# First input transfers of one and three tiles, the third column's products in spare PSUM banks, and the gate's scaling by VectorE instead of GpSimd

## The chip, the cores and the metric

The kernel runs on one core of a Trainium2 chip. The metric is device time in microseconds (us), the median of several executions. One further execution is profiled, and all rows below are from it. Engines: PE is TensorE (matmul), PEld its weight load, DVE is VectorE, ACT is ScalarE, POOL is GpSimd, SP is SyncE, which here only issues DMAs. ACTq and SPq in a row are the sequencers that issue DMAs.

## What is computed

One layer of a streaming encoder, on 256 prompt tokens and 128 sample tokens, with a model width of 2048 and a feed-forward width of 5504 (43 columns of 128):

```python
def _swiglu(x, w_gate, w_up, w_down):
    return (jax.nn.silu(x @ w_gate) * (x @ w_up)) @ w_down
...
    x = x + 0.5 * _swiglu(_rmsnorm(x, p['norm_ffn1']), p['w_ffn1_gate'], p['w_ffn1_up'], p['w_ffn1_down'])
    m, ... = _mixer(_rmsnorm(x, p['norm_mix']), conv_buf, h_ssd, h5_re, h5_im, p)
    x = x + m
    x = x + 0.5 * _swiglu(_rmsnorm(x, p['norm_ffn2']), p['w_ffn2_gate'], p['w_ffn2_up'], p['w_ffn2_down'])
```

The mixer holds a state-space group (SSD) and an S5 group, whose small matrices are worked out from its parameters alone.

## The kernel before

All 384 tokens lie in the free dimension; a tile is 128 rows (of the width or of the weights) by 384 tokens, and the width of 2048 is 16 such tiles. To keep float32 precision each product is made of three: both operands are split into a high part (n_h, wh) and a low remainder (n_l, wl), and PE adds wh·n_h, wh·n_l and wl·n_h in one PSUM bank.

`split_unit` (L47) brings up to eight weight tiles: SP issues the transfer into `raw` (four buffers), ACT casts it to `wh` (L55), DVE subtracts to `wl` (L56), three buffers each. `linear` (L74) makes one output column of 128 rows from two such units, with the matmuls at L86 to L88, in a bank of the pool `psm` (four banks, "mm"). A second pool `psa` (four banks, "aux") serves sums of squares and the mixer.

`ffn` (L191) runs over the 43 columns in chunks of 11, 11, 11 and 10 (second feed-forward block: 15, 14, 14). For each column it makes the gate pg and the up product pu, then g = pg·r by DVE (L213), Silu by ACT (L214), g = g·r by POOL (L215), h = pu·g by DVE (L218), and the split of h into hh by ACT (L221) and hl by DVE (L222). After a chunk's columns the 16 down products pd follow. The scale r of the norm is not applied to x but here, since it is known only after all of x has been squared and summed; it comes from `rms` (L124), which the code calls behind column 0.

Column 0 of the first block is made by `first_pair` (L94), gate and up together, while x arrives: in pieces of 1, 1, 2, 4, 4, 4 of the 16 tiles it issues both weights' transfers on SP, then the transfer of as many x tiles by `feed1` (L1007; the first four tiles on ACT's queue, later ones on SP's), has ACT and DVE split x (L164, L165) and the weights (L108, L109), and issues six matmuls for each tile (L113, L115, L117).

With the second chunk the code interleaves side work, which the scheduler begins in the first chunk already: `s5_prepare` (L268): many small DVE operations (L243 to L265, L368 to L373, L420 to L428) and POOL operations that work out the S5 matrices and the table `ph`. It may start behind `late`, which is column 1's multiply on POOL; it begins with a transfer of the parameters `lam`.

The order on each engine is not that of the code: a scheduler sets it at build time from its own estimate of a timeline, and each engine then runs its list in that order.

Of the kernel before, what the change touches and what calls it, by code (L numbers as in the profile page):

```python
# [9 lines left out]
F32 = mybir.dt.float32  # L10
# [4 lines left out]
P = 128  # L15
D = 2048
T = 384
KT = D // P
# [28 lines left out]
def split_unit(c, wsrc, m, k0, nk):  # L47

    nc = c.nc
    raw = c.wst.tile([P, 8, P], F32, tag="raw", name=f"raw_{c.uid}", bufs=4)  # L50
    wh = c.wst.tile([P, 8, P], F32R, tag="wh", name=f"wh_{c.uid}", bufs=3)
    wl = c.wst.tile([P, 8, P], F32R, tag="wl", name=f"wl_{c.uid}", bufs=3)
    c.uid += 1
    nc.sync.dma_start(raw[:, :nk, :], wsrc[m, :, k0 : k0 + nk, :])
    nc.scalar.copy(wh[:, :nk, :], raw[:, :nk, :])  # L55
    nc.vector.tensor_sub(wl[:, :nk, :], raw[:, :nk, :], wh[:, :nk, :].bitcast(F32))  # L56
    return wh, wl


def turned(ap):  # L60

    return ap.rearrange("p (a b) -> p b a", a=2)


def halves(ap):
    return ap.rearrange("p (a b) -> p a b", a=2)


def straight(ps):

    return ps.rearrange("p (b a) -> p a b", a=2)


def linear(c, wsrc, m, k0, nk, xs, name):  # L74

    nc = c.nc
    ps = c.psm.tile([P, 512], F32, tag="mm", name=name)[:, :T]
    done = 0
    nu = -(-nk // 8)
    sizes = [nk // nu + (1 if i < nk % nu else 0) for i in range(nu)]  # L80
    for n in sizes:
        wh, wl = split_unit(c, wsrc, m, k0 + done, n)
        for i in range(n):
            xh, xl = (turned(z) for z in xs[done + i])
            first, last = done + i == 0, done + i == nk - 1
            nc.tensor.matmul(ps, wh[:, i, :], xh, start=first, stop=False)  # L86
            nc.tensor.matmul(ps, wh[:, i, :], xl, start=False, stop=False)  # L87
            nc.tensor.matmul(ps, wl[:, i, :], xh, start=False, stop=last)  # L88
        done += n
        c.tick()  # L90
    return ps


def first_pair(c, wa, wb, m, xs, names, feed):  # L94


    nc = c.nc
    pa, pb = (c.psm.tile([P, 512], F32, tag="mm", name=n)[:, :T] for n in names)
    k0 = 0
    for nk in (1, 1, 2, 4, 4, 4):  # L100
        raw = c.wst.tile([P, 2, 4, P], F32, tag="raw", name=f"raw_{c.uid}", bufs=4)
        wh = c.wst.tile([P, 2, 4, P], F32R, tag="wh", name=f"wh_{c.uid}", bufs=3)
        wl = c.wst.tile([P, 2, 4, P], F32R, tag="wl", name=f"wl_{c.uid}", bufs=3)
        c.uid += 1
        for i, w in enumerate((wa, wb)):
            nc.sync.dma_start(raw[:, i, :nk], w[m, :, k0 : k0 + nk, :])
        feed(k0, k0 + nk)
        last = nc.scalar.copy(wh[:, :, :nk], raw[:, :, :nk])  # L108
        nc.vector.tensor_sub(wl[:, :, :nk], raw[:, :, :nk], wh[:, :, :nk].bitcast(F32))  # L109
        for i in range(nk):  # L110
            xh, xl = (turned(z) for z in xs[k0 + i])
            for j, ps in enumerate((pa, pb)):
                nc.tensor.matmul(ps, wh[:, j, i, :], xh, start=k0 + i == 0, stop=False)  # L113
            for j, ps in enumerate((pa, pb)):
                nc.tensor.matmul(ps, wh[:, j, i, :], xl, start=False, stop=False)  # L115
            for j, ps in enumerate((pa, pb)):
                nc.tensor.matmul(ps, wl[:, j, i, :], xh, start=False, stop=k0 + i == KT - 1)  # L117
        k0 += nk
    for _ in range(4):
        c.tick()  # L120
    return pa, pb, last
# [69 lines left out]
def ffn(c, x, inp, wg, wu, wd, chunks, name, after, beside=None, before=None, feed=None):  # L191
    nc = c.nc
    r = late = None
    with c.tc.tile_pool(name=f"{name}_pool", bufs=1) as pool:
        f0 = 0
        for ci, nf in enumerate(chunks):
            if ci == 1 and beside:
                c.side.append(beside(late))
            hs = []
            for f in range(f0, f0 + nf):  # L200
                if f == 0 and feed:
                    pg, pu, last = first_pair(
                        c, wg, wu, f, inp.parts, (f"{name}_pg{f}", f"{name}_pu{f}"), feed
                    )
                    before(last)
                else:
                    pg = linear(c, wg, f, 0, KT, inp.parts, f"{name}_pg{f}")
                    pu = linear(c, wu, f, 0, KT, inp.parts, f"{name}_pu{f}")
                if r is None:
                    r = inp.scale(D)  # L210
                g = pool.tile([P, T], F32, tag="g", name=f"{name}_g{f}", bufs=2)
                h = pool.tile([P, T], F32, tag="h", name=f"{name}_h{f}", bufs=2)
                nc.vector.tensor_mul(halves(g), straight(pg), halves(r))  # L213
                nc.scalar.activation(g, g, AF.Silu)  # L214
                on_pool = nc.gpsimd.tensor_mul(g, g, r)  # L215
                if f == 1:
                    late = on_pool
                nc.vector.tensor_mul(halves(h), straight(pu), halves(g))  # L218
                hh = pool.tile([P, T], F32R, tag="hh", name=f"{name}_hh{f}", bufs=max(chunks) + 2)
                hl = pool.tile([P, T], F32R, tag="hl", name=f"{name}_hl{f}", bufs=max(chunks) + 2)  # L220
                nc.scalar.copy(hh, h)  # L221
                nc.vector.tensor_sub(hl, h, hh.bitcast(F32))  # L222
                hs.append((hh, hl))
            for m in range(KT):
                pd = linear(c, wd, m, f0, nf, hs, f"{name}_pd{ci}_{m}")
                xm = halves(x(m))
                nc.vector.scalar_tensor_tensor(xm, straight(pd), 0.5, xm, op0=ALU.mult, op1=ALU.add)
                if ci == len(chunks) - 1:
                    after(m)
            f0 += nf  # L230
        c.finish_side()
# [734 lines left out]
def trunk(ctx: ExitStack, tc: tile.TileContext, a, o):  # L966
    nc = tc.nc
    c = Ctx()
# [6 lines left out]
    c.psm = ctx.enter_context(tc.tile_pool(name="psm", bufs=4, space=bass.MemoryType.PSUM))  # L975
    c.psa = ctx.enter_context(tc.tile_pool(name="psa", bufs=4, space=bass.MemoryType.PSUM))

    warm = c.const.tile([P, 2], F32, name="warm")
    nc.vector.memset(warm, 1.0)
    nc.scalar.copy(warm[:, 1:2], warm[:, 0:1])  # L980
    gains = c.const.tile([P, 4, KT], F32, name="gains")
# [21 lines left out]
    with tc.tile_pool(name="xp1", bufs=1, side="right") as xp1:  # L1003
        xa, x = residual(xp1)
        n1 = Normed(c, gains[:, 0, :], "n1")

        def feed1(m0, m1):  # L1007
            (nc.sync if m0 >= 4 else nc.scalar).dma_start(
                xa[m0 // 8][:, m0 % 8 : m0 % 8 + m1 - m0, :], a["x"][:, m0:m1, :]
            )  # L1010
            for m in range(m0, m1):
                n1.split(m, x(m))

        def before1(last):
            with tc.issue_after(last.ins):
                for m in range(KT):
                    squares(c, n1.acc, m, x(m), "n1", nc.vector)
                nc.scalar.dma_start(cst, a["cst"])
                nc.scalar.dma_start(tri, a["tri"])
            nc.gpsimd.tensor_copy(c.supr, tri[:, 0:P])  # L1020
            nc.gpsimd.tensor_copy(c.susr, tri[:, P : 2 * P])
            c.sup, c.sus = c.supr.bitcast(F32), c.susr.bitcast(F32)

        n2 = Normed(c, gains[:, 1, :], "n2")

        def after1(m):
            n2.add(m, x(m))
            nc.gpsimd.dma_start(keep[m], x(m))

        c.every = 3  # L1030
        ffn(c, x, n1, a["wg1"], a["wu1"], a["wd1"], (11, 11, 11, 10), "f1", after1, lambda late: s5_prepare(c, a, late), before1, feed1)
# [14 lines left out]
    def after2(m):  # L1046
# [6 lines left out]
        nc.scalar.activation(x(m), x(m), AF.Copy, scale=gains[:, 3, m : m + 1])  # L1053

    ffn(c, x, n3, a["wg2"], a["wu2"], a["wd2"], (15, 14, 14), "f2", after2)

    v = nc.vector
    ps = c.psa.tile([P, 4], F32, tag="aux", name="n4_ps")
# [4 lines left out]
    var, t, r = q[:, 0, :], q[:, 1, :], q[:, 2, :]  # L1063
# [156 lines left out]
```

## Time and profile before

| | us |
|---|---|
| median of 3 executions | 2622.58 (2621.67 to 2623.46) |
| profiled execution, device time | 2624.0 |
| its span | 2622.2 |
| PE busy | 2570.5 |
| DVE busy | 1387.7 |
| ACT busy | 926.5 |
| POOL busy | 658.8 |

The mean granted clock of PE is 0.991 of full speed. PE is busy in 98% of the span; what the other engines do costs time only where PE waits for it, and the profile's list of waits says where. A timeline row gives the start, the duration, the engine and line, the operation with its tiles (the written one, an arrow, the read ones), and in brackets how long the engine had been idle before and what ended that.

### The profile page before, as it was taken

To read this page: it belongs to the slowest core of one execution; us is meant where nothing else is said; L and a number is where in the kernel's file an instruction comes from. 1 tells how busy PE (TensorE), PEld (TensorE's weight loads), DVE (VectorE), ACT (ScalarE), POOL (GpSimd) and SP (SyncE) were. 2 spreads that over 40 slices of the span, in tenths; PEclk is the share of its full clock that TensorE was granted. 3 is DMA by queue.
4 is the path that set the end of the run, shared out by engine and by line. 5 is a ranking of instruction groups with operands and counts; after the bars stand their busy time and mean duration, and the time that the engine had idled before them with its cause. 6 is when DMAs were issued, how large, how long until landed. Compare 5 with 4: busy or idle time off the path is not lost.

```text
span 2622.2 us, 39628 instructions
## 1 busy us (share of the span) xinstructions
PE 2570.5 (98%) x15873; PEld 2546.2 (97%) x15873; DVE 1387.7 (53%) x1964; ACT 926.5 (35%) x1180; POOL 658.8 (25%) x1012
## 2 busy tenths in 40 slices
PE   8989999999999999999899999999999999999997
PEld 8989999999999999988899999999999999999997
DVE  7744466564444445568878865444344444444443
ACT  6322332223323335332445644333223332233343
POOL 1573283121100003027566531100000010000112
PEclk9999999999999999999999999999999999999998
DMA  6444564454444436467455544444444444444443
GB/s 204 151 129 140 165 200 149 138 160 135 133 127 147 136 121 186 150 163 159 122 170 167 166 151 136 137 136 129 135 139 137 136 130 133 141 137 137 131 133 107
DMA packets 147001, 380.41 MB, mean 145 GB/s; under 512 B 46080, under 2 KB 51360, under 8 KB 146816
## 3 DMA queue, kind: packets, MB, share of 16 engines
q1 hardware_dynamic: 133456, 344.28, 43.3%
q0 software_dynamic: 11344, 30.72, 3.8%
q10 hardware_dynamic: 2016, 2.87, 0.3%
q8 instruction: 124, 2.03, 0.3%
q14 instruction: 61, 0.50, 0.1%
HBM read 354.60 MB, written 20.05 MB: 143 GB/s over the span
## 4 chain that ended last, share of the span: by engine, by line
PE 86%; DVE 6%; POOL 4%; issue 1%; DMA 1%; ACT 1%; SPq 0%; DVEq 0%; ACTq 0%; POOLq 0%
PE f_pd L86 9%; PE f_pd L88 9%; PE f_pd L87 9%; PE f_pg L86 8%; PE f_pg L87 8%; PE f_pg L88 8%; PE f_pu L88 8%; PE f_pu L86 8%; PE f_pu L87 8%; PE p L87 2%; PE p L86 2%; PE p L88 2%; DVE wl L56 2%; PE u L87 1%; PE u L88 1%
## 5 line engine op out<-in xcount | busy, mean ns | idle before, releaser
L55 ACT CAST wh<-raw 128x1024 fp32r<-128x1024 f32 (+3 forms) x668 | 658.4, 986 | 1450.9 <-PE f_pd L87 417.2
L56 DVE TENSOR_TENSOR wl<-raw,wh 128x1024 fp32r<-128x1024 f32 (+3 forms) x668 | 788.5, 1181 | 678.9 <-ACT wh L55 672.0
L88 PE MATMUL f_pu<-n_h,wl 128*128 128x384 f32 x1360 | 445.7, 328 | 8.1 <-DVE wl L56 8.1
L215 POOL TENSOR_TENSOR f_g<-f_g,n_r 128x384 f32<-128x384 f32 x86 | 130.4, 1516 | 1271.7 <-ACT f_g L214 1271.6
L86 PE MATMUL f_pd<-f_hh,wh 128*128 128x384 f32 x1376 | 448.1, 326 | 0.0
L87 PE MATMUL f_pd<-f_hl,wh 128*128 128x384 f32 x1376 | 448.1, 326 | 0.0
L88 PE MATMUL f_pd<-f_hh,wl 128*128 128x384 f32 x1376 | 448.1, 326 | 0.0
L86 PE MATMUL f_pg<-n_h,wh 128*128 128x384 f32 x1360 | 445.0, 327 | 2.6 <-DVE f_g L213 2.6
L86 PE MATMUL f_pu<-n_h,wh 128*128 128x384 f32 x1360 | 445.5, 328 | 0.0
L87 PE MATMUL f_pu<-n_l,wh 128*128 128x384 f32 x1360 | 445.1, 327 | 0.0
L87 PE MATMUL f_pg<-n_l,wh 128*128 128x384 f32 x1360 | 444.1, 327 | 0.0
L88 PE MATMUL f_pg<-n_h,wl 128*128 128x384 f32 x1360 | 444.0, 326 | 0.0
L88 PEld LDWEIGHTS f_pu<-n_h,wl 128*128 128x128 f32 x1360 | 258.5, 190 | 8.7 <-DVE wl L56 8.7
L86 PEld LDWEIGHTS f_pg<-n_h,wh 128*128 128x128 f32 x1360 | 257.5, 189 | 3.0 <-issue 2.9
L87 PEld LDWEIGHTS f_pd<-f_hl,wh 128*128 128x128 f32 x1376 | 260.0, 189 | 0.0
L88 PEld LDWEIGHTS f_pd<-f_hh,wl 128*128 128x128 f32 x1376 | 260.0, 189 | 0.0
L86 PEld LDWEIGHTS f_pd<-f_hh,wh 128*128 128x128 f32 x1376 | 260.0, 189 | 0.0
L86 PEld LDWEIGHTS f_pu<-n_h,wh 128*128 128x128 f32 x1360 | 258.5, 190 | 0.1
L87 PEld LDWEIGHTS f_pu<-n_l,wh 128*128 128x128 f32 x1360 | 258.4, 190 | 0.1
L87 PEld LDWEIGHTS f_pg<-n_l,wh 128*128 128x128 f32 x1360 | 257.6, 189 | 0.1
L88 PEld LDWEIGHTS f_pg<-n_h,wl 128*128 128x128 f32 x1360 | 257.6, 189 | 0.0
L218 DVE TENSOR_TENSOR f_h<-f_pu,f_g 128x384 f32<-128x384 f32 x86 | 47.8, 556 | 163.2 <-PE f_pu L88 121.4
(481 smaller groups left out, 3133.0 us busy)
## 6 DMA issues: line engine op xcount, KB each, us to landing
raw<-in_wg_dram SPq DMA_DIRECT2D x170, 512.0 KB, 3.6
raw<-in_wu_dram SPq DMA_DIRECT2D x170, 512.0 KB, 3.6
raw<-in_wd_dram SPq DMA_DIRECT2D x80, 448.0 KB, 3.4
raw<-in_win_dram SPq DMA_DIRECT2D x64, 512.0 KB, 4.0
raw<-in_wd_dram SPq DMA_DIRECT2D x80, 320.0 KB, 3.0
raw<-in_wd_dram SPq DMA_DIRECT2D x48, 384.0 KB, 3.2
raw<-in_wout_dram SPq DMA_DIRECT2D x32, 512.0 KB, 3.8
raw<-in_wd_dram SPq DMA_DIRECT2D x16, 512.0 KB, 3.5
```

The costliest lines, as they stand in the source:

```text
L55: nc.scalar.copy(wh[:, :nk, :], raw[:, :nk, :])
L56: nc.vector.tensor_sub(wl[:, :nk, :], raw[:, :nk, :], wh[:, :nk, :].bitcast(F32))
L86: nc.tensor.matmul(ps, wh[:, i, :], xh, start=first, stop=False)
L87: nc.tensor.matmul(ps, wh[:, i, :], xl, start=False, stop=False)
L88: nc.tensor.matmul(ps, wl[:, i, :], xh, start=False, stop=last)
L215: on_pool = nc.gpsimd.tensor_mul(g, g, r)
L218: nc.vector.tensor_mul(halves(h), straight(pu), halves(g))
```

## The change

Three edits. `first_pair` takes its tiles in pieces of 1, 3, 4, 4, 4. `linear` has a parameter `spare`, by which its bank comes from `psa`; the gate and the up product of column 2 in the first feed-forward block use it. The multiply g = g·r is on DVE instead of POOL, in both blocks, and `late` is now a POOL copy of one element per row of g, behind it, into the constant tile `warm`.

```diff
-def linear(c, wsrc, m, k0, nk, xs, name):
+def linear(c, wsrc, m, k0, nk, xs, name, spare=False):
...
-    ps = c.psm.tile([P, 512], F32, tag="mm", name=name)[:, :T]
+    pool, tag = (c.psa, "aux") if spare else (c.psm, "mm")
+    ps = pool.tile([P, 512], F32, tag=tag, name=name)[:, :T]
...
-    for nk in (1, 1, 2, 4, 4, 4):
+    for nk in (1, 3, 4, 4, 4):
...
-                    pg = linear(c, wg, f, 0, KT, inp.parts, f"{name}_pg{f}")
-                    pu = linear(c, wu, f, 0, KT, inp.parts, f"{name}_pu{f}")
+                    pg = linear(c, wg, f, 0, KT, inp.parts, f"{name}_pg{f}", feed and f == 2)
+                    pu = linear(c, wu, f, 0, KT, inp.parts, f"{name}_pu{f}", feed and f == 2)
...
-                on_pool = nc.gpsimd.tensor_mul(g, g, r)
+                nc.vector.tensor_mul(g, g, r)
                 if f == 1:
-                    late = on_pool
+                    late = nc.gpsimd.tensor_copy(c.warm[:, 0:1], g[:, 0:1])
...
-    warm = c.const.tile([P, 2], F32, name="warm")
+    warm = c.warm = c.const.tile([P, 2], F32, name="warm")
```

Behind L76 the changed kernel's lines stand two further on (L213 is L215 there, L218 is L220), and the multiply on DVE is its L217.

The order on PE stays the same throughout. ACT's list in the opening: xp_x are the x tiles, n_h their high parts, and the numbers behind names only tell buffers apart. Before:

```order
L1008 DMA xp_x_102<-in_x_dram 128x384 x2
L108 CAST wh_112<-raw_111 128x2x128
L1008 DMA xp_x_102<-in_x_dram 128x768
L164 ACTIVATE n_h_117<-xp_x_102,gains 128x384
L164 ACTIVATE n_h_135<-xp_x_102,gains 128x384
L108 CAST wh_130<-raw_129 128x2x128
L164 ACTIVATE n_h_153<-xp_x_102,gains 128x384
L164 ACTIVATE n_h_157<-xp_x_102,gains 128x384
L108 CAST wh_148<-raw_147 128x2x256
```

And the same stretch of ACT's list in the changed kernel:

```order
L1010 DMA xp_x_102<-in_x_dram 128x384
L1010 DMA xp_x_102<-in_x_dram 128x1152
L110 CAST wh_112<-raw_111 128x2x128
L166 ACTIVATE n_h_117<-xp_x_102,gains 128x384
L166 ACTIVATE n_h_135<-xp_x_102,gains 128x384
L166 ACTIVATE n_h_139<-xp_x_102,gains 128x384
L166 ACTIVATE n_h_143<-xp_x_102,gains 128x384
L110 CAST wh_130<-raw_129 128x2x384
```

Both transfers of x now stand ahead of the first cast, and the second cast stands behind the splits of tiles 1 to 3.

DVE's list at column 4's up product (wl is its first unit's low part; t, m, wr and wi are side work; f_h is the product of column 3). Before:

```order
L261 TENSOR_TENSOR t_5_2553<-lpi_2591,qi_2621 128x32
L264 TENSOR_TENSOR t_6_2554<-lpi_2591,qr_2620 128x32
L420 TENSOR_TENSOR m_50_3688<-cb_3568,qr_2620 128x64
L421 TENSOR_TENSOR m_51_3689<-cb_3568,qi_2621 128x64
L422 TENSOR_TENSOR m_52_3690<-cb_3568,qr_2620 128x64
L423 TENSOR_TENSOR m_53_3691<-cb_3568,qi_2621 128x64
L262 TENSOR_TENSOR wr_2637<-wr_2637,t_5_2553 128x8x4
L265 TENSOR_TENSOR wi_2638<-wi_2638,t_6_2554 128x8x4
L218 TENSOR_TENSOR f_h_777<-f_pu_715,f_g_776 128x384
L261 TENSOR_TENSOR t_5_2553<-lpi_2591,qi_2621 128x32
L264 TENSOR_TENSOR t_6_2554<-lpi_2591,qr_2620 128x32
L56 TENSOR_TENSOR wl_850<-raw_848,wh_849 128x1024
```

And around the same split on DVE in the changed kernel, where it is wl_843:

```order
L264 TENSOR_TENSOR wr_2630<-wr_2630,t_5_2546 128x8x4
L220 TENSOR_TENSOR f_h_770<-f_pu_708,f_g_769 128x384
L267 TENSOR_TENSOR wi_2631<-wi_2631,t_6_2547 128x8x4
L56 TENSOR_TENSOR wl_843<-raw_841,wh_842 128x1024
L263 TENSOR_TENSOR t_5_2546<-lpi_2584,qi_2614 128x32
L422 TENSOR_TENSOR m_50_3681<-cb_3561,qr_2613 128x64
L266 TENSOR_TENSOR t_6_2547<-lpi_2584,qr_2613 128x32
L423 TENSOR_TENSOR m_51_3682<-cb_3561,qi_2614 128x64
L424 TENSOR_TENSOR m_52_3683<-cb_3561,qr_2613 128x64
L425 TENSOR_TENSOR m_53_3684<-cb_3561,qi_2614 128x64
```

The ten small operations on t, m, wr and wi, which stood ahead of the split, now stand behind it.

DVE's list at column 9's gate (f_g is the gate's tile, f_h the product, f_hl its low part). Before:

```order
L56 TENSOR_TENSOR wl_1540<-raw_1538,wh_1539 128x1024
L213 TENSOR_TENSOR f_g_1568<-f_pg_1446,n_r 128x384
L56 TENSOR_TENSOR wl_1581<-raw_1579,wh_1580 128x1024
L56 TENSOR_TENSOR wl_1611<-raw_1609,wh_1610 128x1024
L218 TENSOR_TENSOR f_h_1569<-f_pu_1507,f_g_1568 128x384
L56 TENSOR_TENSOR wl_1642<-raw_1640,wh_1641 128x1024
L222 TENSOR_TENSOR f_hl_1575<-f_h_1569,f_hh_1574 128x384
```

And the same stretch of DVE's list in the changed kernel:

```order
L56 TENSOR_TENSOR wl_1533<-raw_1531,wh_1532 128x1024
L215 TENSOR_TENSOR f_g_1561<-f_pg_1439,n_r 128x384
L56 TENSOR_TENSOR wl_1574<-raw_1572,wh_1573 128x1024
L217 TENSOR_TENSOR f_g_1561<-f_g_1561,n_r 128x384
L56 TENSOR_TENSOR wl_1604<-raw_1602,wh_1603 128x1024
L220 TENSOR_TENSOR f_h_1562<-f_pu_1500,f_g_1561 128x384
L56 TENSOR_TENSOR wl_1635<-raw_1633,wh_1634 128x1024
L224 TENSOR_TENSOR f_hl_1568<-f_h_1562,f_hh_1567 128x384
```

The multiply L217 stands between the two splits ahead of f_h; on POOL the same multiply stood in the middle of the operations on ph.

## Rows read from the trace of the kernel before

**Rows 1.** Page, part 1: busy time, share of the span and instructions

```profile
PE 2570.5 (98%) x15873; PEld 2546.2 (97%) x15873; DVE 1387.7 (53%) x1964; ACT 926.5 (35%) x1180; POOL 658.8 (25%) x1012
```

**Rows 2.** PE's waits: line, releaser, us in total, times, longest us

```profile
PE f_pu L88 <- DVE wl L56: 8.1, 2, 5.3
...
PE f_pg L86 <- DVE f_g L213: 2.6, 1, 2.6
```

**Rows 3.** Windows: busy time per engine, granted PE clock, DMA share, GB/s

```profile
core 0: us, PE busy (x) PEld busy (x) DVE busy (x) ACT busy (x) POOL busy (x), PEclk, DMA share, GB/s
0.00:8.30 8.30, 6.99 (x30) 6.33 (x30) 2.35 (x9) 3.39 (x6) 0.34 (x6) 1.00 0.64 163
4.11:10.61 6.50, 3.99 (x18) 3.33 (x17) 1.98 (x4) 1.90 (x4) 0.00 (x0) 1.00 0.87 253
...
13.41:16.82 3.41, 3.41 (x13) 3.41 (x12) 3.41 (x6) 3.00 (x5) 0.00 (x0) 0.50 1.01 333
47.54:50.95 3.41, 3.41 (x13) 3.41 (x12) 2.12 (x4) 0.91 (x3) 3.41 (x4) 0.50 0.41 123
153.36:156.77 3.41, 3.41 (x11) 3.41 (x12) 3.22 (x4) 1.62 (x3) 3.41 (x7) 0.50 0.60 183
190.90:197.73 6.83, 5.92 (x19) 5.92 (x19) 3.79 (x5) 0.52 (x1) 4.32 (x22) 0.50 0.70 220
52.00:57.00 5.00, 5.00 (x33) 5.00 (x32) 3.69 (x16) 1.56 (x2) 1.38 (x3) 1.00 0.49 126
...
82.00:107.00 25.00, 25.00 (x156) 25.00 (x155) 24.42 (x104) 7.57 (x9) 11.85 (x34) 1.00 0.41 131
```

**Rows 4.** Timeline of the opening: start, us, engine, line, operation, [idle before]

```profile
1.24 0.88 ACTq L1008 DMA_DIRECT2D xp_x<-in_x_dram  x2
...
4.11 0.33 ACTq L1008 DMA_DIRECT2D xp_x<-in_x_dram  x1
...
10.63 1.12 ACT L164 ACTIVATE n_h<-xp_x,gains 128x384 fp32r<-128x384 f32 x2 [4.56 <-DMA xp_x<-in_x_dram]
...
12.31 0.43 PE L113 MATMUL f_pg<-n_h,wh 128*128 128x384 f32 x1 [4.21 <-ACT wh L108]
...
15.52 0.53 PE L113 MATMUL f_pg<-n_h,wh 128*128 128x384 f32 x1
```

**Rows 5.** Timeline where the third column begins

```profile
46.91 0.40 PE L86 MATMUL f_pg<-n_h,wh 128*128 128x384 f32 x1 [2.63 <-DVE f_g L213]
...
47.14 1.22 DVE L56 TENSOR_TENSOR wl<-raw,wh 128x1024 fp32r<-128x1024 f32 x1
```

**Rows 6.** DVE's waits over the whole span

```profile
DVE wl L56 <- ACT wh L55: 672.0, 470, 4.5
...
DVE f_h L218 <- POOL f_g L215: 41.7, 9, 10.7
```

**Rows 7.** Timeline of PE and DVE at two gates of the first chunk

```profile
153.35 0.69 PE L88 MATMUL f_pu<-n_h,wl 128*128 128x384 f32 x1 [2.80 <-DVE wl L56]
...
187.40 0.56 DVE L218 TENSOR_TENSOR f_h<-f_pu,f_g 128x384 f32<-128x384 f32 x1 [10.34 <-POOL f_g L215]
187.87 3.88 DVE L56 TENSOR_TENSOR wl<-raw,wh 128x1024 fp32r<-128x1024 f32 x1
...
191.81 0.69 PE L88 MATMUL f_pu<-n_h,wl 128*128 128x384 f32 x1 [5.33 <-DVE wl L56]
```

**Rows 8.** Timeline of DVE and PE at column 4's up product

```profile
83.32 0.72 DVE L261 TENSOR_TENSOR t<-lpi,qi 128x32 f32<-128x32 f32 x1
...
85.35 0.54 DVE L218 TENSOR_TENSOR f_h<-f_pu,f_g 128x384 f32<-128x384 f32 x1
...
86.06 1.21 DVE L56 TENSOR_TENSOR wl<-raw,wh 128x1024 fp32r<-128x1024 f32 x1
...
87.99 0.33 PE L88 MATMUL f_pu<-n_h,wl 128*128 128x384 f32 x1
```

**Rows 9.** POOL's multiply: duration in ns, min/median/max, first and last start

```profile
L215 POOL TENSOR_TENSOR f_g<-f_g,n_r x86: 991/1622/1814, 47.4 to 2488.0; 128x384 f32<-128x384 f32 x86
```

## The prediction

> **What bounds the kernel now.** The page comes first: PE is busy 98% of the span, and the other engines half of it at most [rows 1]. So nothing can be won but PE's own gaps, and what the clock loses behind them. The list of PE's waits, read next, says what is there to win at the change's places: 8.1 us in two waits of the up projection for a weight split of DVE, and 2.6 us once for DVE's first multiply f_g [rows 2]. The third place is the opening, where PE waits 4.21 us for a weight cast of ACT [rows 4]. The windows by stage, read last, show what follows on a gap: behind each of the four PE runs at a granted clock of 0.50, the lower of its two levels (1.2 of 2.4 GHz), for 3.41 us, or 6.83 us behind the longest [rows 3]. At half the clock half of that time is lost: 1.7 us behind a short gap, and 5.92/2 = 2.96 us behind the long one, in which PE was busy for 5.92 us. A gap thus costs its wait and this.
>
> **Third column in the spare banks.** PE is done with column 1 at 46.91 - 2.63 = 44.28, and waits until DVE has read column 0's gate out of its bank [rows 5]. DVE can't read earlier, since the norm's scale r isn't there. In the spare banks columns 0 to 2 need six buffers, and eight are there. PE then goes on at 44.28: the splits of column 2's gate stand ahead of r's chain on DVE, and the first one of its up projection, done at 48.36 [rows 5], is wanted after the gate's 48 matmuls, at 44.28 + 48 x 0.16 = 52.0. This is worth 2.63 + 1.7 = 4.33 us [rows 3, 5]. The second pair of buffers after it (column 3) waits for the first columns' gate, which is over by then.
>
> **The gate's scaling on DVE.** The 86 GpSimd multiplies of 1.62 us median go away [rows 9], and DVE gets 86 more; its next multiply, of the same form, takes 0.56 us [rows 7], so 86 x 0.56 = 48.2 us more on an engine that is busy 53% [rows 1]. What it takes away: GpSimd runs the S5 side work in one line, waits there for DMAs too, and the multiply stands behind them. DVE waited 41.7 us in 9 times for it [rows 6], with weight splits queued behind the waiting multiply f_h, and PE behind these. In two places that reached PE. At 153.35 it had waited 2.80 us, with 1.7 us of clock behind it: 4.50 us [rows 3, 7]. At 191.81 it had waited 5.33 us, for a split that itself took 3.88 us behind f_h, with 2.96 us of clock: 8.29 us [rows 3, 7]. Now g's multiply waits for ACT's Silu alone, and the splits stand on either side of it in the order; both stalls go whole. The wl that follows no longer starts at 187.87 but when its cast is there, several us earlier, so that even a split of 3.88 us is in time.
>
> Elsewhere the 48.2 us cost nothing so long as DVE's idle time covers them. That cover is large: DVE waited 672.0 us in 470 times for a weight cast just ahead of a split [rows 6], 1.4 us each and 5.7 us for the four splits of a column, ten times what a column gets. It is missing in one stretch, the S5 preparation, where DVE is busy 24.42 of 25 us [rows 3].
>
> **A new wait there.** The tightest place is column 4's up projection. Its first wl ran from 86.06 to 87.27, and its first matmul at 87.99 [rows 8]. In the changed order ten small S5 rows stand behind this split that stood ahead of it: 86.06 - 83.32 less the 0.54 of f_h, so 2.2 us [rows 8]. Against that, two or three moved multiplies stand ahead of it, 1.1 us by two of them; DVE's gaps between 52 and 57 (5.00 - 3.69 = 1.31 us) may fill, since the S5 chain starts sooner with g from DVE [rows 3]. The split ends at 87.27 - 2.2 + 1.1 = 86.2, or 84.9 with the gaps filled. PE arrives 4.33 us sooner, at 83.66. The stall is thus 1.2 to 2.5 us; I take 2.0, nearer to the later end since nothing shows that the gaps fill, and 1.7 us of clock behind it: a loss of 3.7 us. The bounds are 0 (nothing late) and 4.33 + 1.7 = 6.0 us (all that PE had gained is waited away). A second such place later in the preparation, at a smaller lead of PE: 0 to 3 us, for which I take 0.5.
>
> **The opening.** Two transfers fewer, and x tiles 1 to 3 in one, issued straight behind tile 0's. Before, tiles 0 and 1 were issued from 1.24 at 0.44 us each, and tiles 2 and 3 at 4.11, behind a cast on ACT's queue; they were used at 10.63, 6.5 us on [rows 4]. Now the large one is issued at 1.7. When it lands no row shows. By bytes: what must have come is the gains (32 KB), four x tiles of 192 KB and four weight tiles of 128 KB, 1312 KB or 1.34 MB, and by 8.30 the kernel before had moved 8.30 x 163 = 1.35 MB [rows 3]. By duration: 6.5 us for 384 KB, scaled to 576 KB, is 9.7 us, so 11.4. I take 8.3, since the transfers share one stream and the order of issue now is the order of need. Then ACT has three splits and a longer cast; two splits and a cast of two thirds of it took 12.31 - 10.63 = 1.68 [rows 4], so some 2.5 us, and PE goes on at 10.8. It has done only tile 0 by then, not tile 1: 18 matmuls are left to tile 4, at 0.16 us each (25 us by 156 [rows 3]) 2.9 us, and 1.7 us of clock behind the gap. Tile 4 starts at 15.4, against 15.52 [rows 4]; but before, 16.82 - 15.52 = 1.30 us at half clock were still to come [rows 3], 0.65 us. The gain is 0.8 us. Its bounds: with the 253 GB/s of 4.11 to 10.61 from 1.7 on [rows 3] the 1.34 MB are there at 7.0, a gain of 2.1 us; landing at 11.4 is a loss of 2.3 us.
>
> The copy for `late` is one element a row on GpSimd beside idle time: nothing. From the mixer on, no engine's order changes but for the multiplies; there half-clock stretches follow on gaps as well, and can begin at other places. That is worth one stretch, 1.7 us, either way, and is counted at nothing.
>
> **The sum:** 4.33 + 4.50 + 8.29 - 3.7 - 0.5 + 0.8 = 13.7 us. The profiled execution took 2624.0 us (span 2622.2), which gives 2610.3; it lies 1.4 us above the median 2622.58, from which the same sum gives **2608.9 us**.
>
> **Rivals.**
> (B) The opening doesn't do what it says: the large transfer lands no sooner than 10.6. Then tile 4 starts at 10.6 + 2.5 + 4.6 = 17.7, which is 2.2 later less 0.65, a loss of 1.5 us in place of a gain of 0.8: 2611.2. For it speaks that x was the last to land before; against it the earlier issue.
> (C) The new wait in column 4 doesn't come, since the gaps fill and the S5 rows slip: 3.7 us more, 2605.2. Against it speaks the busy DVE [rows 3].
> (D) DVE and GpSimd hold each other up. Beside GpSimd's S5 work one split took 3.88 us [rows 7], and others 1.2 [rows 8]. If the moved multiplies are stretched as well in the preparation, two more splits come late by 1.3 us, each with 1.7 us of clock: 6.0 us, 2614.9. The Trainium skill has a rule for this (SBUF — State Buffer, "SBUF: two separate sides"): a VectorE operation with two SBUF inputs and a GpSimd operation that reads SBUF take one pair of ports as an exclusive lock, and the loser stands still for the whole instruction. The moved multiply is of that form (g and r), and the 3.88 us row agrees with it; by the same rule the 86 GpSimd multiplies that go away held DVE's splits up before, so that it speaks for the change outside the preparation. By it the time would be up to 2614.9 or some us under 2608.9; no row parts the two.
> (E) Slower: the moved multiply waits for Silu, which stands on ACT behind casts that wait for PE, and weight splits wait behind it, in every column. It decides against the change from (13.7 + 5.2)/86 = 0.22 us of PE's time per column. With all of the multiply's time on the path, 48.2 us: 2657.1. Against it speaks DVE's idle time of 5.7 us per column [rows 6].
> (F) Near no change: in the two columns of the stalls DVE waits for Silu as long as it did for GpSimd, and 12.8 us are not won: 2621.7. Against it: Silu's result had long been there, and GpSimd was the last [rows 7].
>
> **How the numbers follow.** Forecast 0.43, B 0.17, C 0.13, D 0.17 (0.02 of it beyond 2617.3), E 0.05, F 0.05. The range 2603.5 to 2616.5 holds the forecast with the opening's and the new wait's bounds, B, C and most of D, and leaves out E, F and D's end. A measurement of this kernel tells some 0.2% (5.2 us) from no change. Faster by more than that: 0.43 + 0.17 + 0.13 + 0.15 = 0.88; within it 0.05 + 0.02 = 0.07; slower 0.05.
>
> **What would show it.** In the changed kernel's list of PE's waits the line of f_g is gone, and the line of wl holds one wait of about 2 us near 84 in place of 2.80 and 5.33. DVE's waits for GpSimd at f_h are gone, and no wait of DVE for Silu of several us takes their place. Half-clock stretches stand at the opening and behind 85, but not at 47, 153 and 191. PE goes on in the opening near 10.8, and the third column's first matmul follows on the second's last with no gap. It is wrong where PE's wl waits are many and short (D or E), where PE goes on after 12.3 in the opening (B), or where the gap at 44 is only moved to the next column, which would take back the 4.33 us.

## The result and the profile after

The changed kernel takes 2609.02 us (2604.57 to 2609.52, 4 executions), against 2623.02 us of the kernel before beside it (2621.67 to 2624.14): a ratio of 0.9937, with a 95% interval of 0.9925 to 0.9950. (Each ratio below is to the kernel before, run beside it on the same chip.) The forecast was 2608.9. The profiled execution took 2609.49 us with a span of 2607.7, 14.5 us shorter than before. So the sum came out, in part by luck: three of its terms did not (against the forecast the opening gave 1.2 us more, column 4 cost 3.2 us less, the second place cost 4.8 us more), and they happened to cancel.

The page's first part and PE's waits for the weights' casts and splits, in the changed kernel (line, releaser, us in total, times, longest):

```profile
PE 2562.9 (98%) x15873; PEld 2538.4 (97%) x15873; DVE 1417.5 (54%) x2049; ACT 924.9 (35%) x1179; POOL 535.3 (21%) x928
```

```profile
PE f_pg L90 <- DVE wl L56: 3.5, 1, 3.5
PE f_pg L115 <- ACT wh L110: 2.0, 1, 2.0
...
PE f_pu L90 <- DVE wl L56: 0.2, 1, 0.2
```

Against [rows 1] PE is busy for 7.6 us less with the same matmuls, so fewer of them run at half clock; DVE has 29.8 us more, POOL 123.5 us less. Against [rows 2] the wait for f_g is gone, and so are the 2.80 and 5.33 us for wl. A wait of 3.5 us for wl is new.

PE runs the same matmuls in the same order in both kernels, so the time from start to the same matmul, before minus after, says what has been won by then. Four places beside the one of [rows 5], the kernel before first (timeline of PE: start, us, engine, line, operation):

```profile
51.10 0.33 PE L86 MATMUL f_pg<-n_h,wh 128*128 128x384 f32 x1
...
92.05 0.33 PE L86 MATMUL f_pu<-n_h,wh 128*128 128x384 f32 x1
...
197.41 0.49 PE L87 MATMUL f_pu<-n_l,wh 128*128 128x384 f32 x1
...
420.09 0.33 PE L86 MATMUL f_pg<-n_h,wh 128*128 128x384 f32 x1
```

and the same matmuls of the changed kernel, with column 2's first one ahead:

```profile
42.31 0.33 PE L88 MATMUL f_pg<-n_h,wh 128*128 128x384 f32 x1
...
44.75 0.33 PE L88 MATMUL f_pg<-n_h,wh 128*128 128x384 f32 x1
...
86.25 0.33 PE L88 MATMUL f_pu<-n_h,wh 128*128 128x384 f32 x1
...
178.54 0.33 PE L89 MATMUL f_pu<-n_l,wh 128*128 128x384 f32 x1
...
406.56 0.33 PE L88 MATMUL f_pg<-n_h,wh 128*128 128x384 f32 x1
```

| stretch | won, from the rows | forecast |
|---|---|---|
| opening | 46.91 - 42.31 - 2.63 = 1.97 | 0.8 |
| column 2 and the clock behind it | 51.10 - 44.75 - 1.97 = 4.38 | 4.33 |
| column 4 | 92.05 - 86.25 - 6.35 = -0.55 | -3.7 |
| the two gates, with their clock | 197.41 - 178.54 - 5.80 = 13.07 | 12.79 |
| a later split | 420.09 - 406.56 - 18.87 = -5.34 | -0.5 |
| the rest, to the span's 14.5 | 0.97 | 0 |

**The opening.** In the changed kernel (timeline):

```profile
1.25 0.87 ACTq L1010 DMA_DIRECT2D xp_x<-in_x_dram  x2
...
6.62 1.63 ACT L166 ACTIVATE n_h<-xp_x,gains 128x384 fp32r<-128x384 f32 x3 [1.58 <-DMA xp_x<-in_x_dram]
...
8.43 0.83 ACT L110 CAST wh<-raw 128x768 fp32r<-128x768 f32 x1 [0.19 <-DMA raw<-in_wu_dram]
...
9.32 0.43 PE L115 MATMUL f_pg<-n_h,wh 128*128 128x384 f32 x1 [1.99 <-ACT wh L110]
```

Tiles 1 to 3 of x are there at 6.62, earlier even than the lower bound of 7.0, and PE goes on at 9.32.

**The new wait.** PE, and what DVE did ahead of it, in the changed kernel (m are the side work's products with the transferred tile cb):

```profile
394.28 1.01 DVE L411 TENSOR_TENSOR cl<-cl,u 128x320 f32<-128x320 f32 x1 [5.72 <-POOL cl L407]
...
397.60 0.22 DVE L422 TENSOR_TENSOR m<-cb,qr 128x64 f32<-128x64 f32 x1 [1.20 <-DMA cb<-in_s5cb_dram]
397.74 0.75 DVE L423 TENSOR_TENSOR m<-cb,qi 128x64 f32<-128x64 f32 x1
398.42 0.91 DVE L424 TENSOR_TENSOR m<-cb,qr 128x64 f32<-128x64 f32 x1
...
400.43 1.21 DVE L56 TENSOR_TENSOR wl<-raw,wh 128x1024 fp32r<-128x1024 f32 x1
```

```profile
389.93 1.06 ACT L55 CAST wh<-raw 128x1024 fp32r<-128x1024 f32 x1 [4.64 <-PE f_pg L89]
...
401.69 0.43 PE L90 MATMUL f_pg<-n_h,wl 128*128 128x384 f32 x1 [3.55 <-DVE wl L56]
```

The split could have run from 390.99 on, when its cast was done. DVE works down its list: it stood at cl, for which POOL came late, and then at m, for which a transfer came late. In the kernel before DVE's timeline at the same split reads

```profile
413.59 1.21 DVE L56 TENSOR_TENSOR wl<-raw,wh 128x1024 fp32r<-128x1024 f32 x1
...
414.98 0.23 DVE L420 TENSOR_TENSOR m<-cb,qr 128x64 f32<-128x64 f32 x1
415.12 2.56 DVE L421 TENSOR_TENSOR m<-cb,qi 128x64 f32<-128x64 f32 x1
```

There the split stood ahead of m and was done 2.2 us before its use by PE:

```profile
417.00 0.33 PE L88 MATMUL f_pg<-n_h,wl 128*128 128x384 f32 x1
```

The two lists show the swap, before (L420 to L423 are m):

```order
L213 TENSOR_TENSOR f_g_3969<-f_pg_3771,n_r 128x384
L447 SCALAR_TENSOR_TENSOR tt_3811<-kp_3802,cst,tt_3811 128x4x16
L56 TENSOR_TENSOR wl_3982<-raw_3980,wh_3981 128x1024
L447 SCALAR_TENSOR_TENSOR tt_3811<-kp_3802,cst,tt_3811 128x4x16
L420 TENSOR_TENSOR m_84_4641<-cb_4554,qr_2620 128x64
```

and changed:

```order
L422 TENSOR_TENSOR m_84_4634<-cb_4547,qr_2613 128x64
L423 TENSOR_TENSOR m_85_4635<-cb_4547,qi_2614 128x64
L424 TENSOR_TENSOR m_86_4636<-cb_4547,qr_2613 128x64
L449 SCALAR_TENSOR_TENSOR tt_3804<-kp_3795,cst,tt_3804 128x4x16 x2
L215 TENSOR_TENSOR f_g_3962<-f_pg_3764,n_r 128x384
L425 TENSOR_TENSOR m_87_4637<-cb_4547,qi_2614 128x64
L449 SCALAR_TENSOR_TENSOR tt_3804<-kp_3795,cst,tt_3804 128x4x16
L56 TENSOR_TENSOR wl_3975<-raw_3973,wh_3974 128x1024
```

### The profile page after: what moved, and what is told of

Its sections match the earlier page's. It is cut to its first block, busy times and chain, and to the rows that moved or that the text cites. A ratio compares the mean times of both kernels' runs of the same rounds, so it can differ in the third digit from the quotient of the medians.

```text
span 2607.7 us, 39458 instructions
## 1 busy us (share of the span) xinstructions
PE 2562.9 (98%) x15873; PEld 2538.4 (97%) x15873; DVE 1417.5 (54%) x2049; ACT 924.9 (35%) x1179; POOL 535.3 (21%) x928
## 4 chain that ended last, share of the span: by engine, by line
PE 86%; DVE 6%; POOL 3%; DMA 2%; issue 2%; SPq 1%; ACT 1%; DVEq 0%; POOLq 0%; ACTq 0%
PE f_pd L88 9%; PE f_pd L90 9%; PE f_pd L89 9%; PE f_pg L90 8%; PE f_pg L88 8%; PE f_pg L89 8%; PE f_pu L90 8%; PE f_pu L89 8%; PE f_pu L88 8%; PE p L89 2%; PE p L88 2%; PE p L90 2%; DVE wl L56 1%; PE u L90 1%; PE u L89 1%
## 5 line engine op out<-in xcount | busy, mean ns | idle before, releaser
L56 DVE TENSOR_TENSOR wl<-raw,wh 128x1024 fp32r<-128x1024 f32 (+3 forms) x668 | 782.3, 1171 | 659.0 <-ACT wh L55 652.4
L154 POOL TENSOR_TENSOR n_acc<-n_acc,n_sq 128x384 f32<-128x384 f32 x44 | 54.8, 1246 | 1007.2 <-ACT n_sq L153 1006.8
L229 DVE SCALAR_TENSOR_TENSOR xp_x<-f_pd,xp_x 128x384 f32<-128x384 f32 x112 | 62.3, 557 | 133.4 <-PE f_pd L90 133.4
```

What stands on the lines that cost most here:

```text
L154: (eng or nc.gpsimd).tensor_add(acc, acc, sq)
```

## The experiments

Two questions were open: what each edit brings alone, and whether the new wait is DVE's load (the moved multiplies) or DVE's order. The split with the new wait is that of column 19's gate; three of the expectations call it column 13's, by a wrong count. A lead below is the time by which a run's trace reaches a matmul earlier than the kernel before; the places 51.10, 92.05, 197.41 and 420.09 are those of the rows above, in the kernel before. A trace is one execution, while a ratio rests on all.

**The opening alone.** The kernel before with only

```diff
-    for nk in (1, 1, 2, 4, 4, 4):
+    for nk in (1, 3, 4, 4, 4):
```

> The kernel before with the opening's edit alone (pieces of 1, 3, 4, 4, 4). Theory: the parts add up. In the two traces tile 12's products stand 1.8 us earlier by the end of the opening's half-clock stretch, and nothing else hangs on it: about 2 us faster than before, the waits at 47, 153 and 191 us stay. Rival: the other waits absorb the two us, since they end with r and GpSimd, which don't move: no difference.

Ratio 0.9990 (0.9981 to 0.9999), 2.6 us faster. In its trace the lead is 2.1 us at 51.10, as said. The waits of 153 and 191 stay, but a third one, not expected, appears between them. DVE, POOL and PE there:

```profile
168.80 0.56 DVE L218 TENSOR_TENSOR f_h<-f_pu,f_g 128x384 f32<-128x384 f32 x1 [9.88 <-POOL f_g L215]
```

```profile
164.53 0.10 POOL L462 MEMSET ph<- 128x4 f32 x1 [4.41 <-DMA s_phases<-ph]
...
167.77 1.00 POOL L215 TENSOR_TENSOR f_g<-f_g,n_r 128x384 f32<-128x384 f32 x1
...
170.65 0.43 PE L88 MATMUL f_pu<-n_h,wl 128*128 128x384 f32 x1 [2.04 <-DVE wl L56]
```

The multiply on POOL stood behind a store of ph that POOL waited for. POOL's line is paced by its own transfers, so PE's lead is waited away there: of 2.1 us, 0.5 are left at 197.41. This holds for the profiled execution, which with 2625.01 us is among the slowest of its ten (2620.51 to 2625.58); all ten give 2.6 us, with an interval from 0.3 to 5.0, which fits the theory's 2 us and just leaves out the rival's none.

**Column 2 in the spare banks alone.** The kernel before with `spare` only:

```diff
+    pool, tag = (c.psa, "aux") if spare else (c.psm, "mm")
...
+                    pg = linear(c, wg, f, 0, KT, inp.parts, f"{name}_pg{f}", feed and f == 2)
+                    pu = linear(c, wu, f, 0, KT, inp.parts, f"{name}_pu{f}", feed and f == 2)
```

> The kernel before with column 2 in the spare banks alone. Theory: the wait of 2.63 us and the half clock behind it (1.7 us) go, 4.3 us faster, and no wait for DVE's split comes at 84, since the S5 rows keep their place: PE's lead of 4.3 us there is taken from a slack of 0.7 to 1 us in the kernel before, so a small wait of up to 3 us with its half clock is the danger. Rival: that wait comes and takes the gain back, 0 to 1 us faster.

Ratio 0.9989 (0.9980 to 0.9998), 2.9 us faster. In its trace the lead is 4.8 us at 51.10 (0.2 of it from the opening, which this edit leaves as it was) and 3.8 at 92.05, behind a wait of 0.45 us for column 4's split. Between 150 and 192 there are three waits for wl instead of two, 10.1 us in 4 times over the span, and at 197.41 the lead is 3.1:

```profile
PE f_pu L89 <- DVE wl L56: 10.1, 4, 4.2
```

So neither the theory nor its rival: the small wait at column 4 came and with what follows it took 1.0 us, POOL's gates took 0.8 more, and about 3 us are left, by the trace as by the time.

**Both, without the gate's edit**, by the two diffs above together.

> The changed kernel without the gate's edit: opening and column 2 alone, the multiply on GpSimd. Theory: the 6.3 us that these two give PE by 51 us are mostly waited away between 150 and 195, since f_h waits there for GpSimd, whose S5 line is paced by its own transfers and comes no earlier: 2 to 4 us faster than before by the end, so that the gate's edit is worth more on top of the two than alone. Rival: the parts add up, 6.3 us faster than before.

Ratio 0.9980 (0.9971 to 0.9989), 5.2 us faster by time, which alone doesn't part 4 from 6.3. In the trace the lead is 5.3 us at 51.10 and 3.2 us at 197.41, and DVE's wait for POOL is longer than in [rows 6]:

```profile
DVE f_h L219 <- POOL f_g L216: 45.0, 9, 11.4
```

So in this execution 2.1 us were waited away, as the theory had it. By time the two edits alone, 2.6 and 2.9 us, add up to the 5.2 of both within the intervals, so that they lose by POOL's waits is not shown for all executions.

**The gate's multiply on DVE alone.** The kernel before with only

```diff
-                on_pool = nc.gpsimd.tensor_mul(g, g, r)
+                nc.vector.tensor_mul(g, g, r)
...
-                    late = on_pool
+                    late = nc.gpsimd.tensor_copy(c.warm[:, 0:1], g[:, 0:1])
```

> The kernel before with the gate's multiply on DVE alone. Theory: 12.8 us won at 153 and 191, and the wait of 3.5 us with its half clock (5.2 us in all) near column 13's gate appears here too, since in this kernel's order too DVE's four multiplies on cb stand ahead of that weight split: 7.6 us faster. Rival: that wait comes from the lead of 6 us that the other two edits give PE; then it is absent or short here and the gain is 11 to 12.8 us.

Ratio 0.9962 (0.9948 to 0.9975), 10 us faster, with executions from 2609.86 to 2619.93 us, of which the last is the profiled one. The time doesn't part the theory's 7.6 us from the rival's 11; the trace does. In it the two gates give 13.1 us, and the wait at column 19's gate is there without the lead of the other edits:

```profile
PE f_pg L88 <- DVE wl L56: 3.4, 1, 3.4
```

So that wait comes with this edit, not with the lead of the other two. By time the three edits alone sum to 15.5 us, against 16.5 us of all three together by their ratio.

**Load or order.** The changed kernel with the multiply on DVE for the first chunk only:

```diff
-                nc.vector.tensor_mul(g, g, r)
+                (nc.vector if feed and f < 11 else nc.gpsimd).tensor_mul(g, g, r)
```

> The changed kernel, with the gate's multiply on DVE in the first 11 columns only and on GpSimd in all others, as before. In its order the four multiplies on cb stand behind the weight split again. Theory (the order at this one split costs 5.2 us, the other 75 moved multiplies win nothing): the wait of 3.5 us at 401 is gone, about 5 us faster than the changed kernel, near 2604. Rival (DVE waits for GpSimd in later columns would cost PE too): as the changed kernel or slower.

Ratio 0.9926 (0.9913 to 0.9940), 19 us faster than before. In this build m stands behind the split again, and DVE and PE read

```profile
393.70 1.22 DVE L56 TENSOR_TENSOR wl<-raw,wh 128x1024 fp32r<-128x1024 f32 x1
...
395.50 0.23 DVE L422 TENSOR_TENSOR m<-cb,qr 128x64 f32<-128x64 f32 x1 [0.38 <-DMA cb<-in_s5cb_dram]
...
397.28 0.33 PE L90 MATMUL f_pg<-n_h,wl 128*128 128x384 f32 x1
```

The wait is gone; DVE still waits for cb, with nothing urgent behind it. But this build takes load and order away together, so by itself it doesn't part them. Two runs do. First the load doubled, in the changed kernel:

```diff
                 nc.vector.tensor_mul(g, g, r)
+                g2 = pool.tile([P, T], F32, tag="g2", name=f"{name}_gg{f}", bufs=1)
+                nc.vector.tensor_mul(g2, g, r)
```

> The changed kernel with a second multiply of the same form per column on DVE, whose result nothing reads: 86 x 0.56 = 48.2 us more of DVE work. Theory: DVE's idle time covers it, save in the S5 preparation, where the weight split of column 4 ended 0.06 us ahead of its use: a wait of 0.5 to 2 us there with 1.7 us of half clock, perhaps another at 401 as before; 2 to 6 us slower than the changed kernel. Rival: the multiply stands in the path of every column: up to 48 us slower.

Ratio 0.9939 (0.9924 to 0.9954), against 0.9938 (0.9921 to 0.9955) of the changed kernel on the same chip: no difference, neither the theory's 2 to 6 us nor the rival's 48. The page, DVE's waits and PE's:

```profile
PE 2562.4 (98%) x15873; PEld 2538.1 (97%) x15873; DVE 1467.9 (56%) x2135; ACT 924.4 (35%) x1179; POOL 535.2 (21%) x928
```

```profile
DVE wl L56 <- ACT wh L55: 604.5, 481, 4.0
...
PE f_pg L90 <- DVE wl L56: 3.5, 1, 3.5
```

DVE is busy 50.4 us more, its waits for casts shrink from 652.4 to 604.5 us, and PE sees none of it: the wait at column 19 is the same 3.5 us. Even the wait at column 4 that the theory expected didn't come. DVE and PE there:

```profile
78.35 1.22 DVE L56 TENSOR_TENSOR wl<-raw,wh 128x1024 fp32r<-128x1024 f32 x1
...
81.44 0.33 PE L90 MATMUL f_pu<-n_h,wl 128*128 128x384 f32 x1
```

In this build the scheduler put more S5 rows behind the split: it is done 1.9 us ahead of its use, with more load than before.

Second, the cause of the delay taken away at the same load, by another buffer for cb:

```diff
-            cb = t("cb", (P, 4, 4, 16))
+            cb = t("cb", (P, 4, 4, 16), bufs=2)
```

> The changed kernel with two buffers for cb instead of one, so that its transfer can start a round earlier; the four multiplies on cb still stand ahead of the weight split of column 13's gate. Theory: the split was late since the multiplies waited 1.20 us for cb and ran stretched (0.75 and 0.91 us) beside GpSimd; with cb there in time the split ends at some 399.3 instead of 401.6, so the wait of 3.5 us shrinks to 1 us or goes, 2.5 to 5 us faster than the changed kernel. Rival: DVE's work load itself makes the split late; then the wait stays at 3 us or more.

In the trace DVE no longer waits for cb, the split at column 19 starts at 397.98 instead of 400.43, and PE's wait there falls to about 0.1 us. Of the 3.5 us by which the wait is shorter, 2.45 are the earlier split; for the rest PE came there 1.0 us later. For in this build column 4's split starts 1.13 us later than in the changed kernel, and PE now waits there:

```profile
81.56 0.22 DVE L422 TENSOR_TENSOR m<-cb,qr 128x64 f32<-128x64 f32 x1
81.69 0.22 DVE L423 TENSOR_TENSOR m<-cb,qi 128x64 f32<-128x64 f32 x1
81.83 1.22 DVE L56 TENSOR_TENSOR wl<-raw,wh 128x1024 fp32r<-128x1024 f32 x1
...
83.10 0.43 PE L90 MATMUL f_pu<-n_h,wl 128*128 128x384 f32 x1 [1.22 <-DVE wl L56]
```

The two m rows that now stand ahead of it are 0.27 us of the 1.13; 0.83 were there at the split before it, and why is not shown. The time is 0.9940 (0.9926 to 0.9955): a gain over the changed kernel, of which the theory had 2.5 to 5 us, is not shown by it. What is shown is the mechanism at column 19: the wait follows what stands ahead of the split in the list and when that can run, not the load.

**The changed kernel once more**, without an edit.

> The changed kernel once more, beside the other three on their chip. Theory: near 14 us faster than before; the wait at 401 hangs on when a transfer lands, so it may be 5 us shorter in some executions, and the spread is wider than that of the kernel before. Rival: the wait is as long in every execution, and the spread is as small as that of before.

Ratio 0.9938, as at first. Its wait at column 19 was 1.84 us, not 3.55, since POOL issued the transfer of cb at 393.57 instead of 395.23:

```profile
400.09 0.43 PE L90 MATMUL f_pg<-n_h,wl 128*128 128x384 f32 x1 [1.84 <-DVE wl L56]
```

So the wait does differ from one execution to the next. That it widens the spread is not borne out: these four lie within 2.89 us, the seven of the kernel before beside them within 4.62.

**Only x ahead.** The changed kernel with the weights' old pieces, and x's transfers of one and three tiles both ahead:

```diff
-    for nk in (1, 3, 4, 4, 4):
+    for nk in (1, 1, 2, 4, 4, 4):
...
+            elif m0 == 0:
+                nc.scalar.dma_start(xa[0][:, 0:1, :], a["x"][:, 0:1, :])
+                nc.scalar.dma_start(xa[0][:, 1:4, :], a["x"][:, 1:4, :])
```

> The changed kernel with the weights of the opening in pieces of 1, 1, 2, 4, 4, 4 as before, and x as one and three tiles, both issued ahead of the first cast. Theory: the gain of the opening comes from x's transfer, which lands near 6.6 instead of 10.6; PE then goes on some 0.3 us sooner than at 9.32, since the next cast holds one tile, and the time is that of the changed kernel within 1 us. Rival: the weights in one piece of three are what helps; then the gap of 2 us in the opening grows by 1 us or more, and its gain of 2 us is gone.

Ratio 0.9935 (0.9920 to 0.9950): the same time. PE goes on at 8.40 and stops again at tile 4:

```profile
8.40 0.43 PE L115 MATMUL f_pg<-n_h,wh 128*128 128x384 f32 x1 [0.93 <-ACT wh L110]
...
12.68 0.43 PE L115 MATMUL f_pg<-n_h,wh 128*128 128x384 f32 x1 [0.99 <-ACT n_h L166]
```

It is x's early transfer that pays; a smaller piece of weights shortens the first wait and moves it to the next transfer. Column 19's gate waits in this build too, 2.28 us.

**The faster version**: the kernel with the multiply on DVE for the first chunk once more, and then with x ahead as well, by its diff and the one above.

> The kernel with the gate's multiply on DVE in the first 11 columns only, once more, beside the others on this chip. Theory: 18 to 20 us faster than before, with no wait for a weight split at column 13's gate; 4 to 5 us faster than the changed kernel by their ratios to before. Rival: the first result was one chip's, and it is within 2 us of the changed kernel.

Ratio 0.9924 (0.9911 to 0.9936), so by the ratios twice 19 to 20 us faster than before, against 16 to 17 us in the two measurements of the changed kernel, and again no wait at column 19. That is 3 to 4 us between them, less than the 4 to 5 expected (by the medians 19 to 20 against 14 to 17).

> The kernel with the gate's multiply on DVE in the first 11 columns only, and besides the weights of the opening in pieces of 1, 1, 2, 4, 4, 4 with x as one and three tiles ahead. Theory: within 1 us of that kernel without the second edit, since the opening's weight pieces moved the start of the second column by half a us only; about 18.5 to 20 us faster than before. Rival: the order of DVE's S5 work in this build differs again at column 4 and brings a wait of 1 to 3 us with its half clock.

Ratio 0.9917 (0.9903 to 0.9930): the fastest, by an amount that lies within the intervals. Its median is 2.0 us below that of the kernel without the second edit, where the theory had 1; its profiled execution took 2608.60 us, the other four 2602.50 to 2603.35, so its trace can't say where the difference lies. Both beat the kernel before; that they beat the changed one, as their ratios say, is likely, but the intervals overlap.

## Why the prediction was right, and where it was not

**Column 2**: 4.38 against 4.33. Banks, splits and the half clock were as read.

**The gates**: 13.07 against 12.79. As said, no wait for Silu took GpSimd's place, so that F fell. Whether this edit also keeps what the other two bring is open: in the traces 2.1 of their 5.3 us are gone by 197.41 without it, and 0.6 of 6.4 with it, but by time the parts add up.

**DVE's idle time as cover**: right, and gate_twice shows it with twice the load. E fell: no time was lost for 48.2 us of DVE work, nor for twice as much. DVE's busy time rose by 29.8 us only, so its other operations took less than before; the weight splits are 6.2 us of that (788.5 to 782.3 us).

**Column 4**: the step that failed is "the split ends at 86.2, or 84.9", and with it the 3.7 us. It ended at 81.92, 5.35 us earlier than before, for a wait of 0.17:

```profile
80.70 1.22 DVE L56 TENSOR_TENSOR wl<-raw,wh 128x1024 fp32r<-128x1024 f32 x1
...
81.97 0.43 PE L90 MATMUL f_pu<-n_h,wl 128*128 128x384 f32 x1 [0.17 <-DVE wl L56]
```

Of the 5.35 us, 1.71 are an earlier start of the S5 chain: its first row stands at 50.78 here and at 52.49 before, since with the opening's gain r is there earlier. The other 3.65 are a shorter way from that row to the split, here before and changed (windows; the third busy time is DVE's, the fifth POOL's):

```profile
52.49:86.06 33.57, 33.57 (x209) 33.57 (x208) 32.26 (x133) 10.48 (x14) 11.44 (x12) 1.00 0.44 132
```

```profile
50.78:80.70 29.92, 29.92 (x186) 29.92 (x186) 27.80 (x124) 8.31 (x12) 4.58 (x7) 1.00 0.46 149
```

DVE is busy for 4.46 us less on it, and idle for 2.12 us instead of 1.31. So the gaps did not fill, and in that the prediction was right; what it left out are the earlier start and the rest of the shorter work. Beside the ten rows (2.2 us) one weight split fewer lies on this way, and other rows took less, while POOL beside them was busy for 4.58 us instead of 11.44; that POOL is the cause is not shown. The moved multiplies cost 0.94 us. Rival C's time came, or nearly (0.55 us were lost instead of 3.7), but not by its cause.

**The second place**: the step "0.5 of 0 to 3 us" was too small. It took 3.55 us and the half clock, 5.3 us in all (in the execution of changed_again 2.1 us). It also rested on the wrong cause: the prediction looked for places where DVE is full and PE's lead smaller, and the wait came at a lead of 19 us, where DVE was idle for 5.72 us. The order of both kernels showed the four rows on cb changing places with a split; only the first 107 us and the gates were read that closely.

**The opening**: 1.97 against 0.8, since the transfer landed at 6.62. The step that failed is "I take 8.3": the bytes were summed as if all had to come before x, but the weights of tiles 1 to 3 could land behind it, and did, at 8.4. Rival B fell with it.

**Rival D**: what it says of rows is there, what it says of time is not. The side work's m took 0.91 us at 398.42 beside POOL's multiply, and 0.22 without:

```profile
398.50 0.74 POOL L408 TENSOR_TENSOR u<-cb,lpi 128x320 f32<-128x320 f32 x1
```

But the moved multiplies themselves ran at 0.551 us median, 1.090 at most. The Trainium skill (SBUF — State Buffer, "SBUF: two separate sides") states that a VectorE operation with two SBUF inputs and a GpSimd operation that reads SBUF contend for one pair of ports, which the one that starts first holds until it is done. The row agrees by its end, since m ended at 399.33 and POOL's multiply at 399.24. The 0.75 us of the m row ahead of it are not covered by that: POOL then ran no multiply, but the issue of a transfer, 0.93 us from 397.55.

**The last 0.97 us** of the table came late: at the matmul that starts at 2596.69 before and at 2583.05 in the changed kernel the lead is 13.64 us, 0.11 more than at 420.09, and the rest lies behind it, in the last norm and the stores. That the mixer in between gave next to nothing holds for this execution; in changed_again it took the lead from 16.7 to 14.9 us, and no run was made on it.

## What to carry to other kernels

Where one engine does urgent work (a weight split that the matmuls wait for) and side work in one list, what matters is not how busy it is but what stands ahead of the urgent work, and whether that waits for another engine or a transfer: 86 more multiplies cost nothing, four rows of 0.2 us behind a transfer cost 5 us in one execution and 2 us in another. After any edit that lets a scheduler order anew, compare the lists at every urgent item, above all where the engine is idle. And take operations that PE hangs on off an engine that waits for its own transfers: here that gave 13 us at two gates.

## What the runs showed of the hardware

The clock did not fall behind every wait of PE, as the prediction had assumed with its 1.7 us each. Behind the 1.22 us of cb_two_buffers, the 1.84 us of changed_again and the 2.28 us of x_ahead_only it stayed at full; behind the 2.04 us of alone_pieces and the 3.55 us of the changed kernel it was at the lower level (windows: busy time of each engine, then the granted clock; the kernels in this order):

```profile
84.00:87.40 3.40, 3.40 (x23) 3.40 (x22) 3.30 (x19) 0.00 (x0) 0.00 (x0) 1.00 0.64 184
```

```profile
401.10:404.80 3.70, 3.70 (x25) 3.70 (x24) 0.92 (x1) 0.00 (x0) 0.59 (x1) 1.00 0.79 240
```

```profile
400.83:404.24 3.41, 3.41 (x23) 3.41 (x22) 1.51 (x3) 0.50 (x1) 0.59 (x1) 1.00 0.72 210
```

```profile
171.62:175.03 3.41, 3.41 (x13) 3.41 (x11) 2.32 (x3) 0.70 (x2) 3.41 (x8) 0.50 0.85 271
```

```profile
403.05:406.46 3.41, 3.41 (x13) 3.41 (x12) 0.57 (x1) 0.00 (x0) 0.34 (x1) 0.50 0.88 261
```

So the length of a wait alone does not say whether the clock falls. Nor does it say for how long: behind the 3.42 us of alone_gate the clock was at 0.50 from 407.47 to 414.30, behind the 5.39 us of pieces_and_spare only from 189.67 to 193.08. The 1.7 us of the prediction are one outcome, not the price of every gap.

A wait cut from 3.55 to 1.84 us gave back more than its 1.7 us: changed_again is ahead of the changed kernel by 1.60 us at the matmul that waited, and by 3.28 us behind the half-clock stretch (403.28 against 406.56).
